# Paired products in the second layer of an MLP's first chunk, and low weight parts made by a negated copy and an adding transfer

## The chip, the cores and the metric

One Trainium2 chip, one core of it. The kernel is a single program on that core, and the metric is its device time in microseconds (us), the median of several runs. Smaller is better. The core has TensorE (PE, matrix products; loads of its weights are shown as PEld), VectorE (DVE), ScalarE (ACT), GpSimd (POOL), a queue engine for transfers (SP), and 16 DMA engines that all queues share. SBUF is the working memory of 128 partitions, PSUM (8 banks) is where products accumulate.

## The reference, cut to what matters

One transformer layer over 640 tokens (128 context and 512 latent) of width 1024, all in float32:

```python
h  = rmsnorm(x, n1) * (1 + scale1) + shift1
q, k, v, ..., gate_A, gate_B = split(h @ w_in)          # 1024 -> 4352
A, B = grouped_query_attention(...), neighbourhood_attention(...)
m  = sigmoid(gate_A) * (A @ w_br_a) + sigmoid(gate_B) * (B @ w_br_b)
x  = x + gate1 * (m @ w_out)
h2 = rmsnorm(x, n2) * (1 + scale2) + shift2
x  = x + gate2 * (square(relu(h2 @ w_mlp_in)) @ w_mlp_out)   # 1024 -> 4096 -> 1024
y  = rmsnorm(x, final_g)
```

The shifts, scales and gates come from `silu(cond) @ w_mod`, another map of 1024 to 6144 values.

## The kernel before

**Numbers.** The products need more precision than one pass of TensorE gives, so every operand is split into a high part (a rounded copy, type `fp32r`) and a low part (the value minus its high part), and each product is three matmuls: high by high, high by low, low by high (`gemm_k`, L300 to L302). Activations lie with features on partitions and the 640 tokens along the row, in two halves of 320 (`HALVES`, h = 0 and 1). A weight tile is 128 output features by 1024 inputs, 512 KB. It is loaded by SP into a staging tile `st` (`NST` = 3 of them), ACT copies it to `hi` (L257), and DVE or POOL subtracts to make `lo` (L262, L260; the keys in `WPOOLSET` go to POOL). There are three `hi` and three `lo` tiles, so a weight is made ready while the two ahead of it are being used; `Weights.done` frees one and `ahead` converts the next.

**Stages, in order of time.** Norm and first projections; attention, with more of the input projection filled in between; the merge (from 332 us in the trace: gate columns 18 to 33 of `w_in`, and `w_br`); the output projection; the second norm in two halves; then the MLP in four chunks of 1024 hidden features, c = 0 to 3.

**Chunk 0** is done plainly: layer 1 (`w1` 0 to 7) and layer 2 (`w2` 0 to 7) each take 8 tiles x 2 halves x 8 slices of the contraction x 3 = 384 matmuls of 320 columns. `relu2` makes the hidden tiles (with a low part by DVE, L1189), `add_gated` adds the second layer's result to the residual `X1`.

**Chunks 1 to 3** use pairs: two output tiles by two halves of the tokens are a 2 x 2 block problem (contraction halves as the inner pair), solved by seven block products (A11, A12, S1 to S4, A22) instead of eight, in Winograd's way. For each layer and each of four pairs n that is 7 x 4 slices x 3 = 84 matmuls, 336 for a layer. The sums of weight blocks are formed by transfers that add (`accum_op`, L1308 and L1327, on POOL's queue) and then split by ACT and DVE (L1323, L1324); the sums of activations for layer 1 are formed once for all chunks by `t_pieces`, for layer 2 per chunk by `operand` and `t_raw`. `SEQ` lists the products by hand, `Operands` prepares their weights up to six ahead, `layer2` adds each product where it belongs, and `fold(n)` adds the odd tile's shared sum later, in the next chunk's layer 1.

**Around the change.** The modulation vectors of later stages are made by DVE in `late_mods`: 32 tiles of `w_mod` (`wmt`, 512 KB each, three buffers) are loaded by POOL's queue, and 128 multiply-and-sum instructions (L1018) run as fillers. `mod_pace` hands them out: one of 64 steps for each `MCOST` ns of assumed spare time. From the merge on, DVE's order is the written one (`manual`), until the end of chunk 0; the other engines' order is set by a planner from estimated costs. `side` is a list of small jobs of which one or two are taken at each product; during layer 2 of chunk 0 it holds `t_pieces`.

Of the kernel before, what the change touches and what calls it, by code (L numbers as in the profile page):

```python
# [27 lines left out]
WPO = 4  # L28
WP1 = 3
KPOOL = 0  # L30
# [3 lines left out]
QD = 0  # L34
QG = 1
LASTO = (0, 2, 1)
NG = 2
MCOST = 1600
LAG = (0, 4)
# [14 lines left out]
BLKPOOL = (("A12", "A22"), ())  # L54
AUTO = 1
LAG3 = 5
SQP = 0
FINP = ()
HALVES = (slice(0, HT), slice(HT, NT))
# [3 lines left out]
def trunk_layer(ctx: ExitStack, tc: tile.TileContext, xT, small_in, wmodA, wmodB, tabs, cacheK, cacheV, bias,  # L63
# [138 lines left out]
    def w_order():  # L202
        for n in AFILL:
            yield ("in", n), w_in[n]
        for n in BFILL:
            yield ("in", n), w_in[n]
        for n in range(KT):
            for key, src in ((("in", 18 + n), w_in[18 + n]), (("in", 26 + n), w_in[26 + n]), (("br", n), w_br[n])):
                if key[0] == "br" or key[1] not in GATES:
                    yield key, src  # L210
        for n in range(KT):
            yield ("out", n), w_out[n]
        for n in range(KT):
# [15 lines left out]
    class Weights:  # L229
# [15 lines left out]
        def conv(self):  # L245
            self.feed()
            key = self.order[self.nc][0]
            self.busy -= 1
# [7 lines left out]
            for ks in (slice(0, 4), slice(4, KT)) if key[0] == "in" else (slice(0, KT),):  # L256
                ACT.activation(hi[:, ks], st[:, ks], AF.Copy)  # L257
            if key in WPOOLSET:
                for ks in (slice(0, 4), slice(4, KT)) if key[0] == "in" else (slice(0, KT),):
                    nc.gpsimd.tensor_sub(lo[:, ks], st[:, ks], r32(hi[:, ks]))  # L260
            else:
                DVE.tensor_sub(lo, st, r32(hi))  # L262
# [742 lines left out]
    def late_mods():  # L1005
# [228 lines left out]

    hid = [(v_tile("hidh"), v_tile("hidl")) for _ in range(KT)]
    Wt = {}
    for n in range(3):
        Wt[n] = W.get("w1", n)
    first = units([(Wt[n], 0) for n in range(3)], H2, 6)
    for n, h in [(i, h) for h in range(2) for i in range(4)] + [(i, h) for i in range(4, KT) for h in range(2)]:  # L1240
        if n not in Wt:
            Wt[n] = W.get("w1", n)
        ps = first.pop(0) if first else unit(Wt[n], H2, h)
        if h:
            W.done("w1", n)
        relu2(hid[n], ps, h)
        flush_later(posts)
        if not side:
            mod_pace(1600)
    mod_step(64 - lm_n[0])  # L1250
# [4 lines left out]
    FIRST1 = [("A11", 0), ("A22", 0), ("S3", 0), ("S3", 1), ("A22", 1), ("A12", 0), ("A11", 1), ("S2", 0), ("A12", 1),
              ("S1", 0), ("S2", 1), ("S3", 2), ("S4", 0), ("A22", 2), ("S1", 1), ("A11", 2), ("S4", 1), ("A12", 2),
              ("S2", 2), ("S3", 3), ("S1", 2), ("A22", 3), ("A11", 3), ("S4", 2), ("A12", 3), ("S2", 3)]  # L1260
# [16 lines left out]
    class Operands:  # L1277
# [16 lines left out]
        def feed(self):  # L1294
            while self.nl < len(self.loads):
# [49 lines left out]

    OPS.append(Operands())
    Wt = {n: W.get("w2", n) for n in range(2)}
    first = units([(Wt[n], 0) for n in range(2)], hid, 6)
    for n, h in [(0, 0), (1, 0), (0, 1), (1, 1)] + order(KT, 0)[4:]:
        if n not in Wt:  # L1350
            Wt[n] = W.get("w2", n)
        ps = first.pop(0) if first else unit(Wt[n], hid, h)
        if h:
            W.done("w2", n)
        add_gated(n, ps, h, 3)
    while side:
        side.pop(0)()
    flush_later()

    if AUTO:  # L1360
        manual.close()
    v_pool.close()
    m = ctx.enter_context(tc.tile_pool(name="ops", bufs=1, side="right", reuse_waits="tile"))
    banks.close()
    pp8 = ctx.enter_context(tc.tile_pool(name="pp8", bufs=1, space=bass.MemoryType.PSUM, reuse_waits="tile"))
    neg = parts[:, 1]
    DVE.tensor_scalar(neg[:, 24:32], mods[:, 24:32], -1.0, None, op0=OP.mult)
# [128 lines left out]
    def layer2(c, n, o, b, p):  # L1496
        if c < 3:
            if o == "A11":
                WS[n] = tp1.get()
                ACT.activation(WS[n], b, AF.Copy)  # L1500
                gate_half(2 * n, b, 1)
            elif o == "S3":
# [25 lines left out]
        if o == "S4":  # L1528
            gate_half(2 * n, b, 1, neg)
            done_half(2 * n, 1)  # L1530

    OPS[0].ahead()
    for x in SEQ:
# [83 lines left out]
def _host(i):  # L1617
# [60 lines left out]
```

## Time and profile before

| what | value |
|---|---|
| median of 3 runs | 950.52 us (949.47 to 950.79) |
| the profiled execution's own time | 951.01 us |
| its span, first to last instruction | 949.2 us |
| PE busy | 923.6 us, 97% of the span |
| DVE, ACT, POOL busy | 690.0, 542.9, 251.7 us |
| granted clock of TensorE, mean | 0.998 |

Times of a row are those of one profiled execution. Busy time of an engine is the time in which at least one of its instructions ran; matmuls overlap, so the sum of their durations is more than PE's busy time. Layer 1 of chunk 0 runs in this trace from about 527 to 583 us, layer 2 of chunk 0 from 583 to 639, the two layers of chunk 1 from 639 to 738, of chunk 2 from 738 to 837.

### The profile page before, as it was taken

How to read it: one execution, taken by the hardware profiler on the slowest of the kernel's cores; microseconds unless marked ns; L12 is line 12 of the kernel's file. 1: busy time of each engine (PE TensorE's matmuls, PEld its weight loads, DVE VectorE, ACT ScalarE, POOL GpSimd, SP SyncE). 2: the span in 40 equal slices, each digit the busy share in tenths (PEclk: the TensorE clock that was granted, in tenths of full speed). 3: DMA queues.
4: the chain of work that ended last, by engine and by line, in shares of the span. 5: the costliest groups of instructions: out<-in, count | busy, mean ns of one | idle time of the engine just before them, and what ended most of it. 6: DMA issues, size and time to landing. Idle time of an engine off the chain costs nothing.

```text
span 949.2 us, 16613 instructions
## 1 busy us (share of the span) xinstructions
PE 923.6 (97%) x6231; PEld 887.5 (93%) x6231; DVE 690.0 (73%) x1401; ACT 542.9 (57%) x1120; POOL 251.7 (27%) x277
## 2 busy tenths in 40 slices
PE   8999899999999999999999999999999999999996
PEld 7799789889999899999999899999999999999995
DVE  4555775756556789788677777764699858986898
ACT  5456676757656774644423664336763567447765
POOL 0353422314331011201132100024323541364130
PEclk9999999999999999999999999999999999999999
DMA  9954310026354256655742154527778977798573
GB/s 343 258 190 136 87 46 26 23 74 167 107 140 134 89 170 192 199 176 178 243 124 89 64 152 159 135 56 167 150 155 180 183 167 165 156 180 187 102 113 112
DMA packets 49602, 136.94 MB, mean 144 GB/s; under 512 B 6209, under 2 KB 9921, under 8 KB 49521
## 3 DMA queue, kind: packets, MB, share of 16 engines
q1 hardware_dynamic: 27408, 83.49, 28.1%
q0 software_dynamic: 20960, 51.07, 26.7%
q8 instruction: 49, 0.80, 0.4%
q10 hardware_dynamic: 1152, 1.31, 0.4%
q14 instruction: 33, 0.26, 0.1%
HBM read 124.57 MB, written 4.60 MB: 136 GB/s over the span
## 4 chain that ended last, share of the span: by engine, by line
PE 74%; DVE 10%; DMA 5%; ACT 5%; issue 3%; POOL 1%; SPq 0%; DVEq 0%; ACTq 0%; POOLq 0%
PE b L1547 8%; PE b L1548 8%; PE b L1549 7%; PE pg L300 7%; PE pg L302 7%; PE pg L301 6%; PE pss L302 4%; PE pss L300 4%; PE pss L301 4%; DMA ms<-wmodA 3%; PE pt L302 3%; PE pt L301 3%; PE pt L300 3%; DVE wb L1324 1%; PE pt L637 1%
## 5 line engine op out<-in xcount | busy, mean ns | idle before, releaser
L1323 ACT ACTIVATE wb<-wsb 128x512 fp32r<-128x512 f32 x120 | 74.8, 628 | 75.2 <-PE b L1549 49.2
L1548 PE MATMUL b<-op,wb 128*128 128x320 f32 x336 | 104.1, 310 | 0.6 <-DVE op L1412 0.4
L1547 PE MATMUL b<-op,wb 128*128 128x320 f32 x336 | 104.2, 310 | 0.2
L1549 PE MATMUL b<-op,wb 128*128 128x320 f32 x336 | 103.8, 309 | 0.0
L1324 DVE TENSOR_TENSOR wb<-wsb,wb 128x512 fp32r<-128x512 f32 x108 | 78.7, 732 | 31.8 <-ACT wb L1323 30.2
L257 ACT ACTIVATE wh<-wst 128x512 fp32r<-128x512 f32 (+1 forms) x92 | 68.0, 765 | 57.7 <-PE pg L301 19.1
L260 POOL TENSOR_TENSOR wl<-wst,wh 128x512 fp32r<-128x512 f32 (+1 forms) x43 | 62.5, 1470 | 118.9 <-ACT wh L257 109.8
L1327 POOL DMA_DIRECT2D wsb<-w x72 | 63.6, 918 | 91.5 <-DVE wb L1324 63.0
L1018 DVE SCALAR_TENSOR_TENSOR mt<-wmt,cb 128x512 f32<-128x512 f32 x128 | 81.4, 686 | 0.0
L576 DVE TENSOR_TENSOR pl<-pt,ph 128x512 fp32r<-128x512 f32 (+2 forms) x80 | 50.8, 635 | 34.9 <-ACT ph L575 30.0
L1548 PEld LDWEIGHTS b<-op,wb 128*128 128x128 f32 x336 | 63.1, 188 | 1.4 <-DVE op L1412 1.4
L1547 PEld LDWEIGHTS b<-op,wb 128*128 128x128 f32 x336 | 63.0, 188 | 1.1 <-DVE x L1455 1.0
L1549 PEld LDWEIGHTS b<-op,wb 128*128 128x128 f32 x336 | 63.1, 188 | 0.0
L262 DVE TENSOR_TENSOR wl<-wst,wh 128x1024 fp32r<-128x1024 f32 x37 | 45.2, 1222 | 22.0 <-ACT wh L257 22.0
L1014 POOL DMA_DIRECT2D wmt<-wmodB x32 | 17.1, 536 | 163.1 <-DVE mt L1018 98.5
L575 ACT ACTIVATE ph<-pt 128x512 fp32r<-128x512 f32 (+2 forms) x80 | 44.1, 552 | 21.7 <-PE pt L637 10.3
L1308 POOL DMA_DIRECT2D wsb<-w x24 | 23.0, 960 | 90.4 <-DMA wsb<-w 70.4
L1547 PE MATMUL b<-t,wb 128*128 128x320 f32 x144 | 44.6, 310 | 0.0
L1549 PE MATMUL b<-t,wb 128*128 128x320 f32 x144 | 44.5, 309 | 0.0
L1548 PE MATMUL b<-t,wb 128*128 128x320 f32 x144 | 44.5, 309 | 0.0
L1455 DVE SCALAR_TENSOR_TENSOR x<-b,parts,x 128x128 f32<-128x128 f32 (+1 forms) x92 | 38.3, 441 | 3.6 <-PE b L1549 1.8
L1323 ACT ACTIVATE wb<-wst 128x512 fp32r<-128x512 f32 x48 | 29.9, 626 | 15.5 <-PE b L1549 9.3
(888 smaller groups left out, 3242.8 us busy)
## 6 DMA issues: line engine op xcount, KB each, us to landing
wsb<-w POOLq DMA_DIRECT2D x96, 256.0 KB, 5.2
wst<-w SPq DMA_DIRECT2D x40, 512.0 KB, 3.6
wmt<-wmodB POOLq DMA_DIRECT2D x32, 512.0 KB, 4.2
wst<-w_in SPq DMA_DIRECT2D x31, 512.0 KB, 4.2
wsb<-w SPq DMA_DIRECT2D x24, 512.0 KB, 3.7
ms<-wmodA SPq DMA_DIRECT2D x16, 512.0 KB, 7.7
x<-xT SPq DMA_DIRECT2D x16, 320.0 KB, 4.6
bt<-bias SPq DMA_DIRECT2D x16, 320.0 KB, 3.3
```

Source lines behind the costliest of these rows:

```text
L257: ACT.activation(hi[:, ks], st[:, ks], AF.Copy)
L260: nc.gpsimd.tensor_sub(lo[:, ks], st[:, ks], r32(hi[:, ks]))
L300: PE.matmul(ps, wh[:, k], xh[:, sl], start=first, stop=False)
L301: PE.matmul(ps, wh[:, k], xl[:, sl], start=False, stop=False)
L302: PE.matmul(ps, wl[:, k], xh[:, sl], start=False, stop=last)
L1018: DVE.scalar_tensor_tensor(t, st[:, q * 512:(q + 1) * 512], 1.0, r32(cb[2 * q + i][:, :512]), op0=OP.mult, op1=OP.mult, accum_out=parts[:, ...
L1323: ACT.activation(w[:, 0:4], t, AF.Copy)
L1324: (nc.gpsimd if o in BLKPOOL[l - 1] else DVE).tensor_sub(w[:, 4:8], t, r32(w[:, 0:4]))
L1327: nc.gpsimd.dma_start(t, self.src(l, c, n, e)[:, 4 * half:4 * half + 4], accum_op=OP.add)
L1547: PE.matmul(b, w[:, k], xh, start=not whole and k == 0, stop=False, skip_group_check=True)
L1548: PE.matmul(b, w[:, k], xl, start=False, stop=False, skip_group_check=True)
L1549: PE.matmul(b, w[:, 4 + k], xh, start=False, stop=o not in ("A11", "S2", "S1") and k == 3, skip_group_check=True)
```

## The change

Chunk 0's second layer becomes paired like those of the other chunks: its products are put ahead of the others in `SEQ` (`FIRST0`, then S3, A22, S2, S1, S4), `w2`'s first chunk is laid out in memory as the others are, and its hidden tiles are the raw ones that `operand` and `t_raw` work on. `t_pieces` moves to layer 1 of chunk 0, except for its last piece, which overwrites `H2` and stays in layer 2; the difference that this piece needs is kept in a temporary (`p2b`). The modulation work must then end by the middle of layer 1 (`pairs_pool`), DVE's written order ends at the start of layer 1 instead of after chunk 0, and the PSUM banks are laid out anew after layer 1. For 17 weight tiles of the merge (`LOSET`: the columns 20, 23, 24, 25, 27, 28, 31, 32, 33 and the eight of `w_br`) the low part is made by an ACT copy with scale -1 and a transfer on POOL's queue that adds the weight from memory. `wmt` is loaded by SP's queue instead of POOL's (`QM`), the low parts of `w1` 0 to 2 go from POOL to DVE (`WP1`), the pace of the modulation is 1500 instead of 1600 (`MCOST`), and for A11 of layer 2 DVE reads ACT's copy instead of PSUM (`GPV`).

```diff
-WP1 = 3
+WP1 = 0
+QM = 1
-MCOST = 1600
+MCOST = 1500
-AUTO = 1
+AUTO = (0, 0)
+TP = 4
+TQ = 2
+P3 = 8
+GPV = 1
+LOACC = (("in", 20, 26), ("in", 27, 34), ("br", 0, 8))
...
-        for n in range(KT):
-            yield ("w2", n), w2[0, n]
...
-            if key in WPOOLSET:
+            if key in LOSET:
+                ACT.activation(lo, r32(hi), AF.Copy, scale=-1.0)
+                nc.gpsimd.dma_start(lo, src.bitcast(F32R).rearrange("p (k n) -> p k n", k=KT), accum_op=OP.add)
+            elif key in WPOOLSET:
...
-            MISC.dma_start(st, wmodB[n])
+            DQ[QM].dma_start(st, wmodB[n])
...
         def p0():
+            if k == 2:
+                mod_step(64 - lm_n[0])
...
+        def p2b():
+            t4[k] = tp2.get()
+            DVE.tensor_sub(t4[k], raw[1][:, L0], raw[2][:, L1])
...
-        for c in range(1, 4):
-            for o, n in FIRST1:
+        for c in range(4):
+            for o, n in FIRST1 if c else ():
                 yield 1, c, n, o
-            for x in FIRST2:
+            for x in FIRST2 if c else FIRST0:
...
-            OPD[c, name] = m.tile([P, 8, HT], F32R, tag="op", bufs=3, name="op")
+            OPD[c, name] = (bp[0].tile([P, 8, HT], F32R, tag="op3", bufs=1, name="op") if len(OPD) % 3 == 2 else
+                            m.tile([P, 8, HT], F32R, tag="op", bufs=2, name="op"))
...
-                gate_half(2 * n, b, 1)
+                gate_half(2 * n, WS[n] if GPV else b, 1)
...
+    side += [q for k in range(4) for p in t_pieces(k)[:TP] for q in (p, lambda: None)[:TQ]]
...
+        relu2r(hid_raw(0, ((11, 12), (21, 22))[e][h])[:, i], ps)
+        mod_pace(1600)
+        if (n, h) == (3, 1):
+            mod_step(64 - lm_n[0])
+            pairs_pool()
+        if i > 1:
+            ks = slice(0, 3) if i == 2 else slice(3, 4)
+            if h == 0:
+                operand(0, ("B11", "B21")[e], ks)
+            elif e:
+                t_raw(0, "T3", ks)
...
+    side += [lambda: None] * P3 + [p for k in range(4) for p in t_pieces(k)[TP:] + [lambda: None]]
...
-        if l == 1 and c > 1 and o == "S2":
+        if l == 1 and o == "S2":
             fold(n)
...
-    w2 = np.concatenate([w2[:1], w2[1:].reshape(3, 4, 2, P, 1024).transpose(0, 2, 1, 3, 4).reshape(3, 1024, 1024)])
+    w2 = w2.reshape(4, 4, 2, P, 1024).transpose(0, 2, 1, 3, 4).reshape(4, 1024, 1024)
```

## Rows read from the trace of the kernel before

**Rows 1.** The page, busy time of each engine: us, share of the span, instructions.
```profile
PE 923.6 (97%) x6231; PEld 887.5 (93%) x6231; DVE 690.0 (73%) x1401; ACT 542.9 (57%) x1120; POOL 251.7 (27%) x277
```
**Rows 2.** Windows: busy us (instructions) of PE, PEld, DVE, ACT, POOL; clock; DMA share, GB/s.
```profile
332.00:465.00 133.00, 132.75 (x904) 132.42 (x904) 112.19 (x282) 72.95 (x149) 17.96 (x34) 1.00 0.59 186
527.00:583.00 56.00, 54.54 (x363) 53.09 (x362) 41.11 (x94) 33.27 (x69) 2.08 (x4) 1.00 0.34 104
583.00:639.00 56.00, 56.00 (x384) 56.00 (x383) 38.96 (x80) 19.53 (x38) 7.35 (x8) 1.00 0.48 127
639.00:689.00 50.00, 49.57 (x337) 49.05 (x336) 29.02 (x48) 33.08 (x66) 20.99 (x20) 1.00 0.71 157
689.00:738.00 49.00, 49.00 (x336) 48.87 (x335) 45.04 (x79) 25.55 (x40) 15.68 (x19) 1.00 0.80 163
738.00:788.00 50.00, 49.89 (x340) 49.62 (x340) 35.79 (x57) 33.08 (x66) 23.05 (x23) 1.00 0.83 178
```
**Rows 3.** Groups by form, 689 to 738 us: busy, mean ns | idle before.
```profile
L1547 PE MATMUL b<-op,wb 128*128 128x320 f32 x108 | 33.5, 310 | 0.0
```
**Rows 4.** Waits of TensorE's weight loads, 500 to 650 us: total, times, longest.
```profile
PEld pt L197 <- ACT sq L189: 1.9, 1, 1.9
```
**Rows 5.** Groups by form of VectorE in chunk 0, 527 to 583 us.
```profile
L1018 DVE SCALAR_TENSOR_TENSOR mt<-wmt,cb 128x512 f32<-128x512 f32 x22 | 14.3, 684 | 0.0
...
L1189 DVE TENSOR_TENSOR hidl<-rl,hidh 128x320 fp32r<-128x320 f32 x15 | 7.3, 490 | 7.3 <-ACT hidh L1182 7.1
```
**Rows 6.** The same in chunk 0, 583 to 639 us.
```profile
L1202 DVE TENSOR_TENSOR t<-t,t 128x320 fp32r<-128x320 f32 x8 | 3.8, 485 | 0.8 <-ACT t L1201 0.8
...
L1207 DVE TENSOR_TENSOR hr<-hh0h,hh0l 128x640 f32<-128x640 f32 x1 | 0.8, 819 | 0.0
```
**Rows 7.** The same in chunk 1, second layer, 689 to 738 us.
```profile
L1455 DVE SCALAR_TENSOR_TENSOR x<-b,parts,x 128x320 f32<-128x320 f32 x9 | 4.9, 546 | 1.3 <-PE b L1549 0.8 <-ACT tp L1500 0.5
...
L1455 DVE SCALAR_TENSOR_TENSOR x<-tp,parts,x 128x320 f32<-128x320 f32 x1 | 0.5, 540 | 0.0
```
**Rows 8.** The same in chunk 1, first layer, 639 to 689 us.
```profile
L1412 DVE TENSOR_TENSOR op<-hid,op 128x960 fp32r<-128x960 f32 x2 | 2.3, 1158 | 0.3 <-ACT op L1411 0.3
```
**Rows 9.** Groups by form of the merge, 332 to 465 us: VectorE, then ScalarE.
```profile
L262 DVE TENSOR_TENSOR wl<-wst,wh 128x1024 fp32r<-128x1024 f32 x19 | 23.2, 1221 | 4.3 <-ACT wh L257 4.3
...
L257 ACT ACTIVATE wh<-wst 128x1024 fp32r<-128x1024 f32 x9 | 9.5, 1059 | 15.5 <-PE pt L301 8.5 <-PE pss L301 6.8 <-PE pg L301 0.2
```
**Rows 10.** Transfers: queues, issues with KB and median us to landing, extremes of one tile.
```profile
q0 software_dynamic: 20960, 51.07, 26.7%
...
wsb<-w POOLq DMA_DIRECT2D x96, 256.0 KB, 5.2
wst<-w SPq DMA_DIRECT2D x40, 512.0 KB, 3.6
wmt<-wmodB POOLq DMA_DIRECT2D x32, 512.0 KB, 4.2
...
L1308 POOL DMA_DIRECT2D wsb<-w x24: 850/874/1212, 590.3 to 886.7; - x24
DMA to landing us min/median/max: 3.4/4.9/9.0
...
DMA to landing us min/median/max: 3.4/3.7/16.1
```
**Rows 11.** Timeline, 512 to 531 us: start, duration, instruction.
```profile
513.02 2.40 POOL L260 TENSOR_TENSOR w<-wst,w 128x1024 fp32r<-128x1024 f32 x1 [5.23 <-ACT w L257]
513.32 2.33 DVE L329 SCALAR_TENSOR_TENSOR hh0l<-xm,parts,hh0h 128x192 fp32r<-128x192 f32 x1 [0.58 <-ACT hh0h L326]
...
529.83 0.42 DVE L329 SCALAR_TENSOR_TENSOR hh6l<-xm,parts,hh6h 128x192 fp32r<-128x192 f32 x1 [0.58 <-ACT hh6h L326]
```
**Rows 12.** Waits of POOL's queue: us in total, times, longest.
```profile
POOL wmt L1014 <- DVE mt L1018: 98.5, 22, 29.1
```

More of the change, by code (lines that the diff above doesn't have):

```diff
@@ L246, in conv @@
             self.feed()
-            key = self.order[self.nc][0]
+            key, src = self.order[self.nc]
             self.busy -= 1
@@ L293, in trunk_layer @@
     EXTRA = {("out", 4), ("w1", 0)}
+    LOSET = {(x, n) for x, a, b in LOACC for n in range(a, b) if x != "in" or n not in GATES}
     W = Weights()
@@ L1191, in relu2 @@
         posts.append(rest)
-    T = [[tt_tile(f"t{i}_{k}") for k in range(4)] for i in range(1, 4)]
+    T = [{}, {}, {}]
     L0, L1 = slice(0, HT), slice(HT, NT)
@@ L1204, in p0 @@
         def p0():
+            if k == 2:
+                mod_step(64 - lm_n[0])
+            for i in range(3):
+                T[i][k] = tt_tile(f"t{i + 1}_{k}")
             for i in range(2):
@@ L1218, in p2 @@
             cut((T[2][k], T[2][k]), raw[0][:, L0], L0, L1)
+        def p2b():
+            t4[k] = tp2.get()
+            DVE.tensor_sub(t4[k], raw[1][:, L0], raw[2][:, L1])
         def p3():
-            DVE.tensor_sub(raw[0][:, L1], raw[1][:, L0], raw[2][:, L1])
-            cut(H2[k], raw[0][:, L1], L1, L1)
+            cut(H2[k], t4[k], L1, L1)
             for t in H2[k + 4]:
                 ACT.activation(t[:, L1], r32(t[:, L1]), AF.Copy, scale=-1.0)
-        return [p0, p1, p2, p3]
+        return [p0, p1, p2, p2b, p3]
     def natural(k0, sl):
@@ L1232, in formed @@
         return lambda k: (T[i - 1][k][:, L0], T[i - 1][k][:, L1])
[L1235 to L1253, printed above, removed]
     FIRST1 = [("A11", 0), ("A22", 0), ("S3", 0), ("S3", 1), ("A22", 1), ("A12", 0), ("A11", 1), ("S2", 0), ("A12", 1),
@@ L1260, in trunk_layer @@
               ("S2", 2), ("S3", 3), ("S1", 2), ("A22", 3), ("A11", 3), ("S4", 2), ("A12", 3), ("S2", 3)]
+    FIRST0 = [("A11", 0), ("A11", 1), ("A11", 2), ("A12", 0), ("A12", 1), ("A11", 3), ("A12", 2), ("A12", 3)]
     FIRST2 = [("A11", 0), ("S1", 3, 1), ("A11", 1), ("S4", 3, 1), ("A12", 0), ("A12", 1),
@@ L1301, in feed @@
                 else:
-                    if self.busy["B"] >= NB:
+                    if not bp or self.busy["B"] >= NB:
                         return
-                    t = bp.tile([P, KT, P], F32, tag="sb", bufs=NB, name="wsb")
+                    t = bp[0].tile([P, KT, P], F32, tag="sb", bufs=NB, name="wsb")
                 nc.sync.dma_start(t, self.src(l, c, n, x == "B"))
@@ L1344, in get @@
             return self.t.pop(x)
[L1346 to L1367, printed above, removed]
+    bp, pp8 = [], []
     def bank():
-        return pp8.tile([P, 512], F32, tag="b", bufs=8, name="b")[:, :HT]
+        return pp8[0].tile([P, 512], F32, tag="b", bufs=8, name="b")[:, :HT]
     class Temps:
@@ L1530, in layer2, with pairs_pool @@
             done_half(2 * n, 1)
+    OPS.append(Operands())
+    v_pool.close()
+    m = ctx.enter_context(tc.tile_pool(name="ops", bufs=1, side="right", reuse_waits="tile"))
+    neg = parts[:, 1]
+    def pairs_pool():
+        mod_pool.close()
+        bp.append(ctx.enter_context(tc.tile_pool(name="pairs", bufs=1, reuse_waits="tile")))
+        DVE.tensor_scalar(neg[:, 24:32], mods[:, 24:32], -1.0, None, op0=OP.mult)
+        OPS[0].feed()
+    t4 = {}
+    side += [q for k in range(4) for p in t_pieces(k)[:TP] for q in (p, lambda: None)[:TQ]]
+    Wt = {}
+    for n in range(3):
+        Wt[n] = W.get("w1", n)
+    first = units([(Wt[n], 0) for n in range(3)], H2, 6)
+    todo = [(i, h) for h in range(2) for i in range(4)] + [(4, 0), (4, 1), (5, 0), (5, 1), (6, 0), (7, 0), (6, 1), (7, 1)]
+    for n, h in todo:
+        if (n, h) == AUTO:
+            manual.close()
+        if n not in Wt:
+            Wt[n] = W.get("w1", n)
+        ps = first.pop(0) if first else unit(Wt[n], H2, h)
+        if h:
+            W.done("w1", n)
+        e, i = n % 2, n // 2
+        relu2r(hid_raw(0, ((11, 12), (21, 22))[e][h])[:, i], ps)
[9 more added lines that the diff above has]
+                t_raw(0, "T3", ks)
+    while side:
+        side.pop(0)()
+    flush_later()
+    manual.close()
+    banks.close()
+    pp8.append(ctx.enter_context(tc.tile_pool(name="pp8", bufs=1, space=bass.MemoryType.PSUM, reuse_waits="tile")))
+    side += [lambda: None] * P3 + [p for k in range(4) for p in t_pieces(k)[TP:] + [lambda: None]]
     OPS[0].ahead()
@@ L1572, in trunk_layer @@
         OPS[0].ahead()
+        flush_later()
         if side:
```

## The prediction

> **What bounds the kernel now.** I read the page first, then the busy time by stage, then the waits of TensorE, and last the groups of VectorE in the stages that the change touches. The page shows PE busy 97% of the span [rows 1]. The windows show where that is no average: in the merge PE is busy 132.75 of 133 us, in chunk 0's second layer 56.00 of 56, in chunk 1's 49.00 of 49, always at full clock [rows 2]. So from the merge on the time is the number of matmuls times their pitch, and what the other engines do matters only where PE is made to wait. The reader is to see two more things. Between 527 and 583 us PE is 1.5 us short of full, and its waits name one wait of 1.9 us there: the ones-matmul of the second norm's second half, waiting for ACT's squares [rows 2, 4]. And DVE, 73% busy on average, is at 45.0 of 49 us in a paired second layer but only at 29.0 of 50 in chunk 1's first layer [rows 1, 2].
>
> **The change part by part: TensorE.** The price of a matmul must be its pitch. A row gives 0.310 us for one [rows 3], but 336 of them fill 49.00 us and 384 fill 56.00 [rows 2]: 0.1458 us each, since two overlap. By the row's duration the sum below would be 14.9 us, twice what it can be. Paired, chunk 0's second layer has 7 products x 4 pairs x 12 = 336 matmuls in place of 384. 48 fewer x 0.1458 = 7.0 us. The page TensorE: Matmul & The Clock Gate of the Trainium skill (Back-to-back issue gap) gives a shorter pitch for a single matmul of bf16 at full clock, 320 / 2.4 + 2.5 = 136 ns, an estimate by which the sum would be 6.5 us; the trace's pitch decides. That layer has no idle time that could have hidden them [rows 2]. No other part of the change removes a matmul.
>
> **VectorE in chunk 0.** This is where the 7 us could be lost, so I add it up. Second layer: it now does what chunk 1's does, 28 low parts, five operands, the sums, the evacuations: 45.0 us [rows 2]. In place of the few leftovers of layer 1 that this window holds, it gets four cuts of the last piece of `t_pieces`, 4 x 0.49 = 1.9 us [rows 6]; I leave the leftovers in as a bound and take 46 us. First layer, now 41.1 us [rows 2]: less 16 hidden low parts x 0.490 = 7.8 [rows 5]; less modulation. By the calls of `mod_pace` 52 of 64 steps are done before layer 1 at 1600, 55 at 1500 (a tile is 2 steps and 4 instructions, so a step is 2 x 0.684): 3 steps or 4.1 us earlier [rows 5], plus about 1.4 us that now falls after 583. More: the operand low parts B11 and B21, 2 x (1.158 + 0.49), and the T3 difference at the same price, together 4.9 us [rows 5, 8]. And the pieces: per k two sums of 0.819 and four differences and three cuts of 0.485, 5.0 us [rows 6]. `side` holds 9 old entries and 32 new ones; layer 1 takes 32, so about the three first k fall in it, 15.1 us, and the last k, 5.0 us, behind it. First layer: 41.1 - 7.8 - 4.1 + 1.4 + 4.9 + 15.1 = 50.6 of 55 us. Second layer: 46 + 5.0 = 51 of 49 us. That is 2 us over, which cannot be done in time. What is late next: the low parts in line behind. Those are made up to six products ahead, 6 x 12 x 0.1458 = 10.5 us, and the eight banks cover as much for the evacuations, so a backlog of 2 us should not reach PE; it is worked off in chunk 1's first layer, where DVE has 21 us free and gets only the folds (12 instructions of at most 0.55, 5 to 7 us) [rows 2, 7]. I take 0 for PE; the bound above is the whole k = 2 as well falling late, 7 us over and all of it waited for.
>
> **The merge's low parts.** 17 x 1.221 = 20.8 us leave DVE, 17 x 1.06 = 18 us come to ACT (73.0 of 133 us busy now) [rows 2, 9]. PE has 0.25 us to win there, so this is worth nothing by itself; it only makes room for the earlier modulation. Its cost is a longer chain: high copy 1.06, negative 1.06, POOL's issue 0.87, then landing [rows 9, 10]. No row shows an adding transfer of 512 KB. From below it is the plain 512 KB one, 3.6 to 4.2 us; the nearest is the adding one of 256 KB, 5.2 in the median; twice that is 10.4; the longest landing of any such tile is 9.0 and of any weight 16.1 [rows 10]. The cover: a weight's tiles come free three weights ahead, so two weights of 48 matmuls, 2 x 7.0 = 14.0 us, run meanwhile. Chain with a landing of 7 us (between one and two of the 256 KB): 10.0 us; with 9.0: 12.0. Both are inside, so I take 0. The transfers also load the DMA engines: 17 x 0.52 = 8.9 MB at the POOL queue's mean of 26.7% x 949.2 / 51.07 = 5.0 us per MB is 44 us over 133, so the share goes from 0.59 to about 0.92 [rows 2, 10]. In the paired layers it is 0.80 with PE full [rows 2]; 0.92 is beyond what they show.
>
> **The smaller edits.** `wmt` on SP's queue: 32 issues. POOL's queue waits 98.5 us for DVE before these loads, once 29.1 [rows 12]; there the new adding transfers would have stood behind them. On SP the weight loads stand behind them instead, and whoever waits for those is ACT's high copy. The loads are placed in the order in which the planner expects their buffers to be free, and a weight's staging tile is filled some two weights (14 us) before its copy against 3.6 to 4.2 us of landing: 0, and a few us if a weight load is once caught behind such a wait. `WP1`: three low parts of 1.22 us come to DVE in the second norm, and what goes away is POOL's 2.40 us ones, under which DVE's instruction of 0.42 took 2.33 and ended with POOL's [rows 9, 11]. Three such blocks of up to 1.9 us against 3.7 us: between -2 and +2 us of DVE in a stretch where PE has one wait of 1.9 [rows 4]; I take 0. `GPV` changes A11's gated sum from one that reads PSUM, 0.546 us, to one that reads SBUF, 0.540 [rows 7]: 0, and at most the blocking just shown, 1.9 us of DVE, for one of the twelve that meets a subtraction of POOL; in the second layers POOL does none. The page SBUF — State Buffer of the Trainium skill (Who interferes with whom) speaks against `GPV`: a DVE instruction with two SBUF inputs and a GpSimd one that reads SBUF exclude each other, and with it A11's sum has two such inputs. By that rule `WP1` = 0 is a gain of the same kind; the blocked row of 2.33 us agrees with it. `AUTO` only lets the planner fill DVE's gaps. The new bank layout costs at most the ACT copy of the last units; eight products lie between.
>
> **Sum.** Against the profile's own execution, 951.0 us (span 949.2 and 1.8 around it): 951.0 - 7.0 = 944.0. The median of the runs is 0.5 lower, 950.5, so the forecast is 943.5 us, 0.74% faster. (0.2%, 1.9 us, is about what this kernel's measurement tells from no change.)
>
> **The rivals.**
> (1) DVE gives the gain back. If k = 2's and k = 3's pieces both fall into the second layer, DVE has 46 + 10 = 56 us for 49, and if its low parts are what PE then waits for, 7 us come back: 950.5; with half of it 947. For it: 92% busy already in chunk 1's window. Against: PE lost nothing there [rows 2], and the lookahead of 10.5 us.
> (2) Slower: the adding transfers land late. It decides when the chain passes 14.0 us, a landing above 11.0. A weight then repeats every half chain, so each us above costs 0.5 us x 17 = 8.5 us. At 12 us of landing: 943.5 + 8.5 = 952; at 13, 960.5. For it: the DMA share near 0.92, and weights that landed after 16.1 us. Against: 9.0 is the longest among the adding tiles, under a share of 0.80 [rows 2, 10].
> (3) More than the matmuls: with POOL out of the second norm and DVE lighter, the 1.9 us wait and the 0.4 us that PE lacks in chunk 1's first layer go too [rows 2, 4]: 941.2.
>
> **How the numbers follow.** Forecast (942 to 946): 0.60. Rival 1: 0.16, half of it above 948.6. Rival 2: 0.10. Rival 3: 0.14. Faster by over 0.2% (below 948.6): 0.60 + 0.14 + 0.08 = 0.82. Within 0.2%: the rest of rival 1, 0.08, and 0.01 of rival 2: 0.09. Slower: 0.09. The range leaves out the top of rival 1, all of rival 2 and the tip of rival 3: 941 to 948.
>
> **What would show it.** Right: 48 fewer matmuls; a stretch of some 49 us of PE at full between chunk 0's first layer and chunk 1, the same pitch; `wl` without a wait of PE in the merge; DVE there about 20 us less busy for the same work, near 95% in chunk 0. Wrong: PE idle before `wl` in the merge (rival 2), before `wb` or operands at the end of chunk 0 (rival 1), or PE waiting for `wh` behind a `wmt` on SP. The wait at the second norm gone would mean rival 3.

## The result, and the profile after

The changed kernel takes 942.49 us in the median of 4 runs (942.19 to 943.49), the kernel before 950.65 on the same chip (4 runs): a ratio of 0.9915, 95% interval 0.9899 to 0.993. The profiled execution took 942.19, its span is 940.2 against 949.2. The forecast was 943.5 in a range of 941 to 948. The total came out; one term that had been set to 0 turned out to decide whether it would.

The page of after, busy time of each engine, answers to [rows 1]:

```profile
PE 915.9 (97%) x6183; PEld 881.3 (94%) x6183; DVE 696.7 (74%) x1433; ACT 567.5 (60%) x1154; POOL 254.7 (27%) x275
```

PE has 48 instructions fewer. The windows of after by stage answer to [rows 2]: the merge, the output projection with the second norm's beginning, layers 1 and 2 of chunk 0, layer 1 of chunk 1.

```profile
332.00:465.00 133.00, 132.59 (x902) 132.06 (x901) 97.64 (x277) 85.70 (x165) 19.31 (x27) 1.00 0.88 252
465.00:527.00 62.00, 62.00 (x422) 61.68 (x421) 51.37 (x129) 22.88 (x42) 9.49 (x4) 1.00 0.45 152
527.00:581.00 54.00, 53.88 (x361) 52.84 (x361) 45.92 (x92) 34.06 (x73) 3.43 (x4) 1.00 0.46 121
581.00:630.00 49.00, 49.00 (x337) 49.00 (x336) 45.46 (x82) 27.40 (x48) 16.66 (x19) 1.00 0.76 165
630.00:680.00 50.00, 50.00 (x344) 50.00 (x343) 36.13 (x56) 32.71 (x67) 21.79 (x22) 1.00 0.84 181
```

Chunk 0's second layer now fills 49 us where it filled 56, at the same pitch (337 matmuls in 49.00 us). Layer 1 has PE at 53.88 of 54 where it was at 54.54 of 56, and in chunk 1's first layer the 0.4 us are gone. In the merge DVE fell from 112.19 to 97.64 us, ACT rose from 72.95 to 85.70 (16 of the 17 negated copies lie in this window), the DMA share rose from 0.59 to 0.88, and PE did not move.

The stage lengths below are worked out from the traces, as distances between the first matmuls of the stages ("rest": from the first matmul behind layer 1 to the last one of a second layer). They carry most of what follows. All are of one profiled execution each, whose own time stands beside the median: the two can be 5 us apart.

| kernel | merge | output projection | layer 1, chunk 0 | rest | profiled, us | median, us |
|---|---|---|---|---|---|---|
| before | 127.3 | 57.4 | 60.1 | 356.1 | 951.01 | 950.65 |
| before, `w1` 0 to 2 on DVE | 127.3 | 57.4 | 58.2 | 358.3 | 951.45 | 948.83 |
| after | 127.7 | 57.4 | 58.1 | 348.8 | 942.19 | 942.49 |
| pairs alone | 127.3 | 57.6 | 64.0 | 348.6 | 947.25 | 948.18 |
| pairs and `WP1` | 127.3 | 57.5 | 58.1 | 349.0 | 942.64 | 942.07 |
| after, the merge's low parts on DVE | 127.3 | 57.4 | 58.0 | 350.1 | 940.75 | 943.06 |
| after, `w1` 0 to 2 on POOL | 128.4 | 57.4 | 63.3 | 348.7 | 947.85 | 948.18 |
| after, DVE's written order | 128.3 | 57.4 | 59.9 | 350.6 | 945.52 | 944.18 |
| after, written order and `w1` 0 to 2 on POOL | 130.4 | 57.4 | 62.9 | 349.9 | 951.48 | 948.85 |
| after, `wmt` on POOL's queue | 141.2 | 57.7 | 58.1 | 349.8 | 955.97 | 950.88 |
| after, pieces in layer 2 | 129.3 | 57.4 | 58.2 | 369.5 | 963.06 | 962.54 |

So after is 7.3 us shorter behind layer 1 (the 48 matmuls and the 0.4 us), 2.0 shorter in layer 1, 0.4 longer in the merge.

The waits of PE and its weight loads in after, 300 to 900 us (total, times, longest), answer to [rows 4]:

```profile
PEld pss L310 <- DMA wl<-w_in: 0.6, 1, 0.6
PEld pg L310 <- DMA wl<-w_in: 0.4, 1, 0.4
PEld pt L203 <- ACT sq L195: 0.5, 1, 0.5
```

The 1.9 us at the second norm became 0.5, and the transfers added 1 us of waits in the merge at most. Where the modulation ran is the part of the profile that was not foreseen. Windows of `mt` on DVE in after (length, busy us and count, in which each instruction's reading of the accumulator counts too, clock, DMA share, GB/s):

```profile
507.00:523.00 16.00, 6.13 (x20) 1.00 0.30 100
523.00:540.00 17.00, 4.52 (x14) 1.00 0.44 125
540.00:560.00 20.00, 0.69 (x2) 1.00 0.72 190
560.00:600.00 40.00, 0.00 (x0) 1.00 0.42 101
```

and the same windows in the kernel before:

```profile
507.00:523.00 16.00, 0.00 (x0) 1.00 0.31 86
523.00:540.00 17.00, 0.00 (x0) 1.00 0.23 76
540.00:560.00 20.00, 3.91 (x12) 1.00 0.18 52
560.00:600.00 40.00, 11.75 (x36) 1.00 0.66 194
```

Before, 15.7 us of modulation ran behind 540 us and none between 507 and 540; now 10.7 us run between 507 and 540 and 0.7 behind.

### The profile page after: what moved, and what is told of

It reads as the page before. It is cut to its first block, busy times and chain, and to the rows that moved or that the text cites. A ratio compares the mean times of both kernels' runs of the same rounds, so it can differ in the third digit from the quotient of the medians.

```text
span 940.2 us, 16705 instructions
## 1 busy us (share of the span) xinstructions
PE 915.9 (97%) x6183; PEld 881.3 (94%) x6183; DVE 696.7 (74%) x1433; ACT 567.5 (60%) x1154; POOL 254.7 (27%) x275
## 4 chain that ended last, share of the span: by engine, by line
PE 76%; DVE 9%; DMA 5%; issue 4%; ACT 4%; POOL 1%; SPq 0%; DVEq 0%; POOLq 0%; ACTq 0%
PE b L1571 10%; PE b L1572 10%; PE b L1573 10%; PE pg L308 6%; PE pg L310 6%; PE pg L309 6%; PE pss L310 3%; PE pss L309 3%; PE pss L308 3%; PE pt L309 2%; PE pt L308 2%; PE pt L310 2%; DMA wl<-w_in 2%; PE pt L645 1%; PE pss L393 1%
## 5 line engine op out<-in xcount | busy, mean ns | idle before, releaser
L1318 ACT ACTIVATE wb<-wsb 128x512 fp32r<-128x512 f32 x140 | 87.1, 628 | 93.4 <-PE b L1573 62.0
L1572 PE MATMUL b<-op,wb 128*128 128x320 f32 x448 | 138.6, 309 | 0.3 <-DVE op L1387 0.2
L1571 PE MATMUL b<-op,wb 128*128 128x320 f32 x448 | 138.6, 309 | 0.3 <-DVE x L1430 0.3
L1573 PE MATMUL b<-op,wb 128*128 128x320 f32 x448 | 138.4, 309 | 0.0
L1319 DVE TENSOR_TENSOR wb<-wsb,wb 128x512 fp32r<-128x512 f32 x128 | 94.9, 745 | 28.4 <-ACT wb L1318 28.2
L1322 POOL DMA_DIRECT2D wsb<-w x84 | 73.2, 901 | 130.1 <-DVE wb L1319 97.6
L267 POOL TENSOR_TENSOR wl<-wst,wh 128x512 fp32r<-128x512 f32 (+1 forms) x41 | 57.1, 1411 | 118.0 <-ACT wh L261 108.9
L261 ACT ACTIVATE wh<-wst 128x512 fp32r<-128x512 f32 (+1 forms) x84 | 59.6, 737 | 46.8 <-PE pg L309 16.3
L1572 PEld LDWEIGHTS b<-op,wb 128*128 128x128 f32 x448 | 84.1, 188 | 0.8 <-DVE op L1387 0.8
L1571 PEld LDWEIGHTS b<-op,wb 128*128 128x128 f32 x448 | 84.1, 188 | 0.8 <-DVE x L1430 0.8
L1573 PEld LDWEIGHTS b<-op,wb 128*128 128x128 f32 x448 | 84.1, 188 | 0.0
L1303 POOL DMA_DIRECT2D wsb<-w x28 | 25.9, 927 | 138.5 <-DMA wsb<-w 47.0
L1430 DVE SCALAR_TENSOR_TENSOR x<-b,parts,x 128x128 f32<-128x128 f32 (+1 forms) x116 | 46.3, 428 | 2.6 <-PE b L1573 1.9
L1387 DVE TENSOR_TENSOR op<-hid,op 128x1280 fp32r<-128x1280 f32 (+2 forms) x32 | 36.9, 1154 | 7.8 <-ACT op L1386 7.7
L1430 DVE SCALAR_TENSOR_TENSOR x<-tp,parts,x 128x320 f32<-128x320 f32 (+2 forms) x60 | 39.2, 680 | 1.0 <-ACT tp L1475 1.0
```

What stands on the lines that cost most here:

```text
L1318: ACT.activation(w[:, 0:4], t, AF.Copy)
L1319: (nc.gpsimd if o in BLKPOOL[l - 1] else DVE).tensor_sub(w[:, 4:8], t, r32(w[:, 0:4]))
L1322: nc.gpsimd.dma_start(t, self.src(l, c, n, e)[:, 4 * half:4 * half + 4], accum_op=OP.add)
L1430: DVE.scalar_tensor_tensor(X1[i][:, sl], src[:, sl.start - off:sl.stop - off], g[:, j:j + 1], X1[i][:, sl], op0=OP.mult, op1=OP.add)
L1571: PE.matmul(b, w[:, k], xh, start=not whole and k == 0, stop=False, skip_group_check=True)
L1572: PE.matmul(b, w[:, k], xl, start=False, stop=False, skip_group_check=True)
```

## The experiments

Edits are against the changed kernel unless another is named. Each run has its own runs of the kernel before beside it; ratios are to those.

**The pairs alone.**

```diff
-WP1 = 0
+WP1 = 3
-QM = 1
+QM = 0
-MCOST = 1500
+MCOST = 1600
-GPV = 1
+GPV = 0
-LOACC = (("in", 20, 26), ("in", 27, 34), ("br", 0, 8))
+LOACC = ()
```

> The changed kernel with only the pairs and what they need; all helpers (low parts by transfer, wmt on SP, w1's low parts on DVE, pace 1500, A11 from ACT's copy) set back. My theory: the 48 matmuls are 7.0 us and need no helper, so 943.5 us against 950.5 before; the remaining 1 to 2 us of the change come from the second norm. Rival: without the helpers DVE cannot do the pieces and the modulation in layer 1 of chunk 0, and 2 to 7 us come back: 945.5 to 950.5, with PE waiting at the end of chunk 0.

Measured 948.18 us (946.53 to 949.04), ratio 0.9964 (0.9951 to 0.9978). The theory that the matmuls alone make the gain falls. The gain is there behind layer 1 (348.6 us, as in after), and 3.9 us of it are lost in layer 1 (64.0 against 60.1). The rival's time came, but not its place: PE waits in the second norm, not at the end of chunk 0.

**`w1` 0 to 2 back on POOL.**

```diff
-WP1 = 0
+WP1 = 3
```

> The changed kernel with the low parts of w1 0 to 2 on POOL again. Theory: the second norm's wait of TensorE shrank from 1.9 to 0.5 us because POOL's subtractions no longer hold DVE there; with them back the wait returns, so 1.4 to 2 us more than the changed kernel: about 944.2. Rival: it shrank because the planner orders DVE now or because the modulation moved; then no difference (942.5) and the wait stays at 0.5 us.

Measured 948.18 (946.52 to 953.06), ratio 0.9975 (0.9962 to 0.9987): 5.7 us above the change where 1.4 to 2 were expected, most of it in layer 1 (63.3 against 58.1). The timeline of this run, POOL and then DVE (start, duration, instruction), shows how:

```profile
517.03 2.63 POOL L267 TENSOR_TENSOR wl<-wst,wh 128x1024 fp32r<-128x1024 f32 x1 [0.78 <-ACT wh L261]
524.97 4.26 POOL L267 TENSOR_TENSOR wl<-wst,wh 128x1024 fp32r<-128x1024 f32 x1 [5.31 <-ACT wh L261]
...
517.32 2.82 DVE L337 SCALAR_TENSOR_TENSOR hh1l<-xm,parts,hh1h 128x128 fp32r<-128x128 f32 x2
527.34 2.44 DVE L1026 SCALAR_TENSOR_TENSOR mt<-wmt,cb 128x512 f32<-128x512 f32 x1
536.67 0.55 DVE L1147 SCALAR_TENSOR_TENSOR x<-pt,parts,x 128x320 f32<-128x320 f32 x1
```

A multiply-and-sum that takes 0.68 us elsewhere takes 2.44 beside POOL's subtraction, and POOL's own, 2.40 in [rows 11], is stretched to 4.26. The last addition to the residual, on which the norm's second half waits, starts at 536.67; in after at 531.69, in before at 533.50. The page SBUF — State Buffer of the Trainium skill (Who interferes with whom) has this rule, that two such instructions exclude each other and that issue order decides who waits; the trace agrees so far as either engine is seen as the one that waits. What PE makes of it, in the windows of this run:

```profile
523.00:530.00 7.00, 6.16 (x36) 5.11 (x36) 7.00 (x18) 4.73 (x10) 4.26 (x1) 1.00 0.00 0
530.00:540.00 10.00, 8.01 (x47) 6.67 (x46) 9.30 (x28) 4.49 (x12) 0.00 (x0) 1.00 0.37 118
540.00:582.00 42.00, 41.58 (x282) 41.02 (x280) 35.28 (x63) 26.47 (x55) 3.43 (x4) 1.00 0.45 123
```

and of after, with one window more ahead of them:

```profile
507.00:523.00 16.00, 16.00 (x108) 15.68 (x107) 16.00 (x50) 9.75 (x20) 0.00 (x0) 1.00 0.30 100
523.00:530.00 7.00, 6.88 (x48) 6.62 (x47) 6.88 (x17) 2.71 (x7) 0.00 (x0) 1.00 0.35 83
530.00:540.00 10.00, 10.00 (x65) 9.22 (x64) 9.85 (x24) 7.32 (x18) 0.87 (x1) 1.00 0.50 154
540.00:582.00 42.00, 42.00 (x288) 42.00 (x287) 33.88 (x63) 27.35 (x58) 2.56 (x3) 1.00 0.48 126
```

36 + 47 + 282 = 365 matmuls against 48 + 65 + 288 = 401: 36 fewer, x 0.1458 = 5.2 us, the difference of the stage lengths (63.3 - 58.1). Ahead of 540 us DVE is all but full in both kernels, so what POOL takes from it is late for the norm. In the kernel before it was not:

```profile
507.00:523.00 16.00, 16.00 (x108) 15.68 (x107) 11.36 (x23) 7.07 (x16) 5.34 (x3) 1.00 0.31 86
523.00:530.00 7.00, 7.00 (x48) 6.77 (x48) 5.82 (x14) 4.34 (x11) 2.41 (x1) 1.00 0.26 85
```

There 4.6 us of the 16 and 1.2 of the 7 were free to take up a block.

**The kernel before, with `w1` 0 to 2 on DVE** (edit against the kernel before).

```diff
-WP1 = 3
+WP1 = 0
```

> The kernel before with only the low parts of w1 0 to 2 moved from POOL to DVE. Theory: the wait of 1.9 us at the second norm goes there too: 948.6 to 949.2, with chunk 0's layer 1 ending 1.4 to 2 us earlier than at 582.4. Rival: the three low parts of 1.22 us on DVE, whose order is written there, cost what POOL's blocks cost: 950.5.

Measured 948.83 (947.2 to 951.45), ratio 0.9979 (0.9967 to 0.9991): 1.8 us, as expected. The profile is of the slowest of the 12 runs: layer 1 is 1.9 us shorter there, and 2.2 us are lost again behind it. The same edit is worth 1.8 us here and 5.7 to 6.1 beside the pairs.

**Pairs and `WP1`, nothing else.**

```diff
-QM = 1
+QM = 0
-MCOST = 1500
+MCOST = 1600
-GPV = 1
+GPV = 0
-LOACC = (("in", 20, 26), ("in", 27, 34), ("br", 0, 8))
+LOACC = ()
```

> The pairs with one helper only, w1's low parts 0 to 2 on DVE; low parts of the merge on DVE, wmt on POOL, pace 1600, A11's sum from PSUM. Pairs alone took 948.2, the whole change 942.5. Theory: the whole difference of 5.7 us is POOL's subtractions in the second norm, so this is 942.5 to 943.5, and chunk 0's layer 1 takes 58 us from its first matmul to layer 2's first instead of 64. Rival: the other helpers carry a part, 945 to 947.

Measured 942.07 (940.8 to 943.48), ratio 0.9913 (0.99 to 0.9927): the whole change. It differs from the pairs alone by `WP1` only, and its layer 1 takes 58.1 us in place of 64.0. So the pairs and `WP1` are enough for the whole gain, as expected.

**The merge's low parts back on DVE.**

```diff
-LOACC = (("in", 20, 26), ("in", 27, 34), ("br", 0, 8))
+LOACC = ()
```

> The changed kernel with the merge's 17 low parts on DVE again (no adding transfers), all else as changed. Theory: PE is full in the merge either way, the transfers only make room on DVE: at most 1 us slower (942.5 to 943.5), DVE in the merge from 98 back to about 112 of 133 us, and the few waits for wl of 0.3 to 0.6 us gone. Rival: the room is needed; DVE falls behind the pace of 1500 and the modulation runs into the second norm and layer 1: 945 or more.

Measured 943.06 (940.01 to 943.19), ratio 0.9901 (0.9885 to 0.9918), the same as the change within the intervals. The merge's window in this run:

```profile
330.00:463.00 133.00, 132.75 (x905) 132.42 (x904) 115.64 (x295) 72.91 (x150) 6.45 (x13) 1.00 0.61 189
```

DVE has 115.64 us where after has 97.64, and PE 132.75 where after has 132.59: the transfers win DVE 18.0 us that nobody waits for.

**A second adding transfer behind each of the 17.** It adds the first of the tile's eight slices once more, so that this slice counts twice in the output.

```diff
                 nc.gpsimd.dma_start(lo, src.bitcast(F32R).rearrange(...), accum_op=OP.add)
+                nc.gpsimd.dma_start(lo[:, 0:1], src.bitcast(F32R).rearrange(...)[:, 0:1], accum_op=OP.add)
```

> The changed kernel with a second adding transfer (one slice of eight, 64 KB) behind each of the 17, into the same low part, so that the weight's first slice is counted twice and the output is another one. It tests the price of a late low part. The chain is now two copies of 1.05, an issue of 0.86 and a landing of 8.0 = 11.0 us; with another issue of 0.86 and a landing of 4 to 5 it is 16 to 17 us, past the cover of 14.0. Theory: a weight repeats every half chain, so (16.5 - 14.0) / 2 x 17 = 21 us slower: 963. Rival: the second transfer only delays the first slice of a weight and the planner or the buffers hide it: less than 5 us.

Measured 971.28 (966.82 to 978.19), ratio 1.0218 (1.0177 to 1.0259): 28.8 us above the change. Its first waits of PE, 300 to 900 us:

```profile
PE pg L311 <- DMA wl<-w_in: 8.2, 2, 7.4
PE pg L311 <- DMA wl<-w_br: 4.7, 2, 3.1
```

The direction holds, and the price was put too low. By the traces the chain (from the start of the negated copy to the last landing, and 1.06 for the high copy) is 10.6 us in the median in after and 16.0 here, as long as expected; it includes up to 6.7 us in which a weight's transfer stands on POOL's queue behind another weight's second one. In the merge, 32.5 us longer in this profile, PE's clock was part of it:

```profile
332.00:497.00 165.00, 141.82 (x899) 139.45 (x898) 97.75 (x277) 85.03 (x163) 33.78 (x41) 0.93 0.79 212
```

PE is 23 us short of full there, and the granted clock averaged 0.93.

**`wmt` back on POOL's queue.**

```diff
-QM = 1
+QM = 0
```

> The changed kernel with wmt loaded by POOL's queue as before. Theory: the adding transfers then stand behind wmt loads that wait for DVE; low parts land late, TensorE waits for wl in the merge, 2 us or more slower: 944.5 or above. Rival: the planner places wmt where it does not wait long, and it costs nothing: 942.5.

Measured 950.88 (946.79 to 957.31), ratio 0.9999 (0.9976 to 1.0021): 8.4 us above the change. The profile is of a slower run (955.97), in which the merge is 13.5 us longer. The waits, of the weight loads in the merge and beyond and of POOL's queue from 330 to 480 us:

```profile
PEld pg L310 <- DMA wl<-w_in: 5.3, 2, 4.2
PEld pt L310 <- DMA wl<-w_in: 4.8, 1, 4.8
...
POOL wmt L1022 <- DVE mt L1026: 40.4, 13, 8.6
```

The landing of `wl` is no longer in the median than in after (7.2 us against 8.0; the longest 10.7 against 9.4). Of the two long stalls the one of 4.8 us, which ends at 433.2, is of the expected kind. ACT has made the negated copy at 419.04, and the transfer is issued at 422.49, 3.5 us later, because `wmt` loads ahead of it wait for DVE to free their buffers [rows 12 show the same queue before]:

```profile
417.99 1.05 ACT L263 ACTIVATE wl<-wh 128x1024 fp32r<-128x1024 f32 x1
...
421.97 0.53 POOL L1022 DMA_DIRECT2D wmt<-wmodB  x1 [1.90 <-DVE mt L1026]
422.49 0.92 POOL L264 DMA_DIRECT2D wl<-w_in  x1
```

The other one, of 4.2 us, is not: its transfer is issued 0.9 us after its copy, but the copy starts at 344.29, where after has it at 342.27. There the planner's order on ACT has changed. The granted clock, 0.70 to 0.87 in the windows of 8 us at both stalls, adds its part.

**The pieces left in layer 2.**

```diff
-TP = 4
+TP = 0
-P3 = 8
+P3 = 0
```

> The changed kernel with all of t_pieces put into layer 2 of chunk 0 again (TP = 0, P3 = 0). VectorE has then about 45.5 + 20 = 65.5 us for 49 us of matmuls there. Theory of the prediction: a backlog is hidden up to the 10.5 us by which low parts are made ahead, the rest is waited for: about 6 us slower than the changed kernel, 948.5. Rival 1 of the prediction at its full price: all 16 us come back, 958.5. Third way: the planner does the pieces earlier or later than written and nothing is lost, 942.5.

Measured 962.54 (960.03 to 963.55), ratio 1.0116 (1.01 to 1.0131): 20.0 us above the change, and above the rival's 958.5 too. The theory of a cushion of 10.5 us falls. Waits of the weight loads, 300 to 960 us, and the windows of layer 2 and of a stretch behind it:

```profile
PEld b L1571 <- DVE tp L1416: 6.8, 4, 4.1
PEld b L1573 <- DVE wb L1319: 4.8, 5, 1.6
PEld b L1571 <- ACT hh2h L1209: 4.0, 1, 4.0
```

```profile
580.00:630.00 50.00, 41.76 (x262) 39.57 (x261) 47.89 (x91) 28.63 (x52) 10.25 (x12) 0.97 0.56 106
...
650.00:666.00 16.00, 11.87 (x71) 11.34 (x70) 13.86 (x22) 7.28 (x15) 8.43 (x9) 0.91 0.74 167
```

PE waits for a PSUM bank that DVE has not read (`tp`), for low parts (`wb`) and for the pieces themselves (`hh2h`), which no weight made ahead can cover. PE stands 8.2 us in the first of these windows and 4.1 in the second, and the granted clock (0.97 and 0.91) costs some 3 us more.

**A11's gated sum from PSUM.**

```diff
-GPV = 1
+GPV = 0
```

> The changed kernel with A11's gated sum reading PSUM again (GPV = 0). Theory: 0.546 against 0.540 us for twelve instructions, no difference: 942.5. Rival, by the rule that two SBUF inputs meet POOL's reads: the change loses by GPV, and without it the kernel is up to 1 us faster: 941.5.

Measured 943.4 (941.98 to 945.73), ratio 0.9921 (0.9907 to 0.9936): no difference from the change. In layer 2 of chunk 0 the six 320-column sums that read ACT's copy average 750 ns in after, 1.2 us of DVE over 545 each, and the two that remain without the edit average 1066: the lost time is there either way, and DVE has room for it. One source is POOL: in after it makes a low part of a paired weight from 623.64 to 625.06, and four of the sums, which start at 623.33, take 2.68 us together.

**DVE's written order kept through layer 1.** `AUTO` is the unit of layer 1 at which the written order ends; (4, 0) is halfway.

```diff
-AUTO = (0, 0)
+AUTO = (4, 0)
```

> The changed kernel with AUTO = (4, 0) and nothing else. Theory, as predicted: with POOL quiet the order of DVE there is worth nothing, 942.5, within 0.5 us. Rival: modulation that is written after the second norm leaves DVE idle in it and late behind it, 944 or more.

Measured 944.18 (941.21 to 945.93), ratio 0.9934 (0.9917 to 0.9951): 1.7 us above the change, the rival's time, but with intervals that overlap. The windows of its profile (945.52):

```profile
507.00:523.00 16.00, 16.00 (x108) 15.68 (x107) 11.14 (x30) 9.70 (x20) 0.00 (x0) 1.00 0.10 34
...
540.00:582.00 42.00, 40.35 (x274) 39.93 (x273) 41.46 (x90) 26.15 (x54) 3.42 (x4) 1.00 0.52 149
```

With the written order DVE has 4.9 us idle in the first window, where it has none in the changed kernel, and then 41.46 of 42 in layer 1, where PE loses 1.65 us. So in this profile the free order earns its time by moving the modulation ahead; that it earns any in the median is not shown.

**Written order, and `w1` 0 to 2 on POOL.**

```diff
-WP1 = 0
+WP1 = 3
-AUTO = (0, 0)
+AUTO = (4, 0)
```

> The changed kernel with w1's low parts 0 to 2 on POOL and DVE's written order kept up to the middle of layer 1 (AUTO = (4, 0)), so that no modulation is put into the second norm ahead of its place. With the planner's order the same took 948.2 and layer 1 took 63.3 us. Theory: POOL's blocks alone cost what they did before (layer 1 of 60.1 us), the rest is the modulation that the planner put in gaps which the blocks had already eaten: 944.5, layer 1 of 60 us. Rival: the blocks alone do it, 948 and 63 us again.

Measured 948.85 (944.96 to 957.07), ratio 0.9985 (0.9965 to 1.0004). The time is the rival's, 948 and 63 us, but it does not decide: the runs lie 12 us apart, and in the profile (951.48) the merge is 2.7 us longer than in after and a fall of the granted clock is in layer 1:

```profile
530.00:540.00 10.00, 8.25 (x47) 7.14 (x47) 6.55 (x13) 4.65 (x11) 1.15 (x1) 0.95 0.29 90
540.00:550.00 10.00, 9.13 (x54) 8.87 (x54) 8.11 (x23) 4.68 (x11) 0.00 (x0) 0.88 0.34 112
```

That clock costs 0.05 x 10 + 0.12 x 10 = 1.7 us, so at full clock layer 1 would have taken about 61.2. What the profile does show is the norm: no modulation runs between 523 and 540 us, and POOL's subtractions and the last addition to the residual read

```profile
516.69 2.41 POOL L267 TENSOR_TENSOR w<-wst,w 128x1024 fp32r<-128x1024 f32 x1 [16.36 <-ACT w L261]
...
537.46 0.55 DVE L1147 SCALAR_TENSOR_TENSOR x<-pt,parts,x 128x320 f32<-128x320 f32 x1
```

The subtractions take 2.41, 2.42 and 2.42 us, as before, and not 4.26. Everything is later by 3.7 us here, so the addition has to be counted from layer 1's first matmul (525.93); it starts 11.5 us behind that, as in the kernel before (11.3), where the run with the planner's order has 13.8.

**The output projection's four low parts on DVE too.**

```diff
-WPO = 4
+WPO = 8
```

> The changed kernel with the last subtractions of POOL in this stretch, the low parts of the output projection's tiles 4 to 7, on DVE as well (WPO = 8): a version that might beat both. Theory: the second norm's wait of 0.5 us is all that is left to win, 942.0 to 942.5. Rival: four more low parts of 1.22 us make DVE late in the output projection, 943.5 or more.

Measured 941.28 (940.42 to 944.37), ratio 0.991 (0.9895 to 0.9924), the same as the change within the intervals. No version ran measurably faster than the change.

## Why the prediction was right, and where its sum was not

**TensorE, 48 x 0.1458 = 7.0 us: right.** The count, the pitch and the place agree; behind layer 1 the trace is 7.3 us shorter, of which 0.3 is the time PE lacked in chunk 1's first layer.

**`WP1`, taken as 0 with bounds of -2 and +2: the step that failed.** It measured -1.8 in the old kernel, at the edge of the bounds, and -5.7 (change against `w1` 0 to 2 on POOL) to -6.1 (pairs and `WP1` against pairs alone) beside the pairs. The bounds came from a second norm in which DVE had idle time: 11.36 and 5.82 us busy in the 16 us and 7 us from 507 in the trace of before. In the paired kernel it is busy all of the 16 us and 6.88 to 7.00 of the 7, and the same blocks make PE wait. Shown: the blocks, the later residual, the 36 matmuls. The traces also show what the modulation adds. Start of the last addition to the residual, in us behind layer 1's first matmul, in eight profiles (no modulation: none runs in the 15 us ahead of that matmul, nor between it and the addition):

| | no modulation in the norm | modulation in the norm |
|---|---|---|
| `w1` 0 to 2 on DVE | 8.5 (before, edited), 8.8 (written order) | 9.4 (after), 9.2 (pairs and `WP1`) |
| `w1` 0 to 2 on POOL | 11.3 (before), 11.5 (written order) | 13.8 (after, edited), 13.7 (pairs alone) |

POOL's three subtractions delay it by 2.7 us without the modulation and by 4.4 to 4.5 with it. That the medians follow is not shown: the run with the written order and POOL's subtractions took 948.85, no less than the one with the planner's order.

**`AUTO` "only lets the planner fill DVE's gaps": right in words, but not the small thing it was taken for.** Filling the gaps is what moves the modulation out of layer 1 and, with POOL's subtractions, what makes the second norm tight. Its own worth, 1.7 us in the medians, is within the noise.

**So the sum hid two errors that cancel; that the total came out is in part luck.** By the profiles it reads: pairs -7.3 behind layer 1 and +3.9 in it, `WP1` -5.9, its excess over +3.9 being the 2.0 us that the norm's wait gave back, and +0.4 in the merge, -8.9 in all for the measured -8.8. The 2.0 us are rival 3, and in the profile it came nearly whole: 951.0 - 7.0 - 2.3 = 941.7 us against 942.19. In the medians 942.49 lies between it and the forecast, 0.3 us above what the profile gave. The same sum for the pairs alone would have missed by 4.7 us.

**VectorE in chunk 0: right that PE loses nothing there, wrong in the placement.** Forecast 50.6 of 55 and 51 of 49 us, with one k of the pieces late; measured 45.92 of 54 and 45.46 of 49. All `t_pieces` but the last fell into layer 1, where only 5.2 us of modulation were left behind 523 us, against 15.7 before. The cushion of 10.5 us that was to cover a backlog did not show: with the pieces, four k of 5.0 us, all in layer 2, 20.0 us were lost. Whether it would have covered the 2 us of the forecast was not tried. By that run rival 1 was priced too low; it did not come for lack of a backlog.

**The merge's low parts, worth 0: nearly right.** Landing 8.0 us in the median and 9.4 at most where 7 was taken, share 0.88 where 0.92 was; the chain, counted as at the second transfer, is 10.6 us in the median and 11.9 at most in the trace, against a cover of 14.0. (The sum 1.05 + 1.05 + 0.86 + 8.0 = 11.0 us counts the issue twice, as the prediction's did: a landing is counted from the start of its issue.) The row of after:

```profile
L264 POOL DMA_DIRECT2D wl<-w_in x9: 852/860/922, 343.6 to 439.9; - x9
DMA to landing us min/median/max: 5.3/8.0/9.4
```

Even so TensorE waits for a late `wl` now and then. The five profiles without adding transfers have a merge of 127.3 us each, and the seven with them, `wmt` on SP and no second transfer, 127.7 to 130.4: a cost of 0.4 us or more, with no gain that a run shows. Rival 2 exists for a longer chain, as the second transfer shows, at a higher price than was put on it (28.8 us for an expected 21).

**`wmt` on SP, 0: right, and more than 0 without it.** With the transfers, POOL's queue costs 8.4 us, one of the two long stalls being the wait that was named. Without them the edit is worth nothing (942.07 with `wmt` on POOL's queue, 943.06 on SP's), so it is the condition for the transfers.

**`GPV` and `MCOST`: 0.** `GPV` was run alone, `MCOST` was not; pairs and `WP1` at 1600 equal the change at 1500. The new bank layout was not undone by itself; PE at 49.00 of 49 leaves it no cost. The prediction's reading that POOL does no subtraction in the second layers was wrong (one of 1.6 us lies between 689 and 738 us before, one of 1.4 us in layer 2 of chunk 0 in after), without a cost that the runs show.

## What to carry to other kernels

Price a blocked or late instruction by the idle time of its engine in the kernel that will run, after all moves, and not in the trace of before; an edit worth 1.8 us alone was worth 6 once the same stretch had been filled. When several edits come together, look for the one that only makes room: the pairs won 7 us and would have kept 2.5 without it. On POOL's queue a load that waited for its buffer held up the transfer behind it by 3.5 us, so a transfer on a tight path belongs on another queue than prefetches.

## What the runs showed of the hardware beyond that

In a long stall of PE the granted clock fell, which made the stall dearer than its length. With `wmt` on POOL's queue, three windows of the merge (length, then PE, PEld, DVE, ACT, POOL, clock, DMA share, GB/s):

```profile
348.00:356.00 8.00, 4.11 (x24) 3.84 (x24) 6.00 (x16) 4.82 (x11) 1.99 (x4) 0.80 1.04 243
356.00:364.00 8.00, 8.00 (x45) 8.00 (x44) 4.98 (x17) 1.61 (x4) 1.08 (x2) 0.78 0.91 297
364.00:372.00 8.00, 8.00 (x57) 8.00 (x56) 5.35 (x15) 4.55 (x9) 1.43 (x2) 1.00 0.82 199
```

PE stood for 3.9 us in the first, was busy all of the second with 45 matmuls where the third has 57, and those 12 cost another 12 x 0.1458 = 1.7 us. The clock has two levels, 1.2 and 2.4 GHz; 0.78 is a mixture over the window. In finer windows of this trace it is 1.00 until 352 us, 0.50 from 354 to 358, and 1.00 again from 360. Not every stall did this: with `w1` 0 to 2 on POOL, PE lost 2.0 us between 530 and 540, in pieces, and the clock stayed at 1.00. Such runs also scatter: 946.79 to 957.31 here, 966.82 to 978.19 with the second transfer, and 942.19 to 943.49 for the change.

The other is the price of an adding transfer of 512 KB: 8.0 us to landing in the median, where plain ones of that size took 3.6 to 4.2 before [rows 10]. Most of this need not be the adding. In the merge of after, where the DMA share is 0.88, the plain loads are slower too (median us to landing in 332 to 465 us, the last number):

```profile
wl<-w_in POOLq DMA_DIRECT2D x9, 512.0 KB, 8.2
wst<-w_in SPq DMA_DIRECT2D x8, 512.0 KB, 5.3
```

`wmt` took 6.0 there, and the six loads of `w_br` 7.8, as long as its adding transfers (7.9). No run tells load and adding apart.
